# Value projections that leave the multiplier token by token, and latents that leave it unscaled

## The chip, the cores and the metric

The kernel runs on one core of one Trainium2 chip. A core has a matrix engine (TensorE, PE in the profile; its weight loads are shown apart as PEld), a vector engine (DVE), an activation engine (ACT), a general engine (POOL), and a queue engine (SP) that issues nearly all transfers. Each engine takes its instructions in a fixed order and stops at one that has to wait. Matrix products land in PSUM, eight banks of 128 x 512 float32; everything else is kept in SBUF or in device memory. The metric is the device time of one execution in microseconds (us); before the change the median of three runs is 2705.36 us (2704.07 to 2706.91).

## The reference

A two-layer encoder on 1024 tokens of width 1024. Each layer normalises x, projects it once, and cuts the columns of the projection among four attention groups; their outputs are concatenated, projected back and added; a squared-ReLU MLP follows. The parts that the change touches:

```
h = rms_norm(x, norm1_g[l]);  proj = h @ w_in[l]       # columns cut into groups A, B, C, D
A: cq (192), ckv (128), kr (32)                        # latents
   q = rms_norm(cq) @ w_uq;  c = rms_norm(ckv);  k_nope = c @ w_uk;  v = c @ w_uv
   softmax(q k) v, 4 heads of 64 + 32 rotary; values of 64
B: q, k (256 each, rotary), v (256 = 4 heads x 64)
   w = softmax(q1 k1) - lam * softmax(q2 k2);  w @ v
C: windowed attention, 4 query heads    D: neighbourhood attention on a 64-wide grid
```

Since `rms_norm` divides every token by its own root mean square (rms), the division may be done after a projection, and for `rms_norm(cq)` it drops out but for the small constant under the root.

## The kernel before

**Layout.** Activations are kept feature-major: a tile has 128 features on the partitions and 1024 tokens along the row. Every float32 operand is split into two parts, high and low (`split`: ACT writes the high part, DVE or POOL subtracts), and a product takes three matmuls: high x high, low x high, high x low (`passes`). In a projection the weights stand still in the array and 512 tokens move (`several`, `product`), so a tile of 128 output features takes 8 x 2 x 3 = 48 matmuls: eight pieces of the contraction, two halves of the tokens, three passes. The input of the projections is x times the gain, without 1/rms; that factor, spread over a tile `rb` along the tokens, is multiplied in when a result leaves PSUM (`ev_plain`), or is part of the rotary tables (`ev_rope`).

**Group B's start.** Two waves of three tiles each (`WAVES`) are projected into six PSUM banks: Q, K and V of heads 0 and 1, then of heads 2 and 3. ACT copies each half to SBUF (L453), which frees the bank. Q and K take a rotary step of three DVE products and a sum, a split into two `both` buffers' worth of parts (a pool of two), and a store to device memory. Attention needs values token-major, so `to_values` turns V: DVE multiplies by `rb`, PE transposes four pieces of 128 tokens into a bank (L642), ACT and DVE split the result, SP stores it. `attn_b` then loads Q, K and V per head (`stack`, `vtile`) and runs the softmax: scores into the `sb` banks (L810), scaling and row minimum on DVE (L812), the exponential on ACT (L815), transposes (L846) and products with V (L834, L835: the value tile stands still, 256 probabilities move).

**Latents.** While group B's attention runs, other work is put between its steps (`weave`, `fill`): `proj_latent` projects the three tiles of group A's latents, multiplies by `rb`, squares for the second norm (ACT, then matmuls against a column of ones, L659) and splits them; then `proj_d` projects group D. Group B's attention, latents and group D's projections all use a pool of two banks `mm`, two `tr`, three `sb` and one `pv`.

**Group A's values.** During group D's attention, `latent_up` projects the latents up; for the values it takes two tiles, each in two halves of 512 tokens (3 matmuls each), multiplies by a spread row `rkv` and turns the result with `to_values`.

**Order.** In the attention part a scheduler orders the instructions of each engine from their dependences and a model of their durations, with `high_priority` for steps of the attention; in the MLP the order of PE is that of the code.

## Time and profile before

| what | value |
|---|---|
| median of three runs | 2705.36 us |
| the profiled execution's own time | 2709.95 us |
| its span, first to last instruction | 2707.9 us |
| mean granted TensorE clock | 0.969 |
| PE, DVE, ACT, POOL busy | 94%, 72%, 53%, 42% of the span |
| layer 0: group B's projections and attention | about 30 to 350 us |
| layer 0: groups D, C and A's way up | about 350 to 480 us |
| layer 0: groups C and A, output projection | about 480 to 690 us |
| layer 0: MLP | about 690 to 1350 us |
| layer 1 | the same again from about 1350 us |

The busy time of PE adds matmuls that overlap, and a matmul's duration is longer than the time until the next one starts; so for what a matmul costs in a stream, the distance of two starts is read. A line such as `L190` is that of a helper (`tt`) and covers many uses; tiles tell them apart. The granted clock is the share of full speed at which the array ran in a stretch.

### The profile page before, as it was taken

The numbers are of one execution on the slowest core, as the hardware profiler recorded it, in microseconds if no ns is written. First come the engines' busy times: TensorE is split into PE (matmuls) and PEld (weight loads), VectorE is DVE, ScalarE is ACT, GpSimd is POOL, SyncE is SP. The second block draws the span as 40 slices with busy tenths as digits, with TensorE's granted clock in tenths as the row PEclk, the third lists the DMA queues.
The fourth block names the chain that finished last, engine by engine and source line by source line (L and its number), as shares of the span: only waits on it lengthen the run. The fifth ranks groups of instructions, "written<-read, shape, count | busy, mean of one in ns | idle before, by whom it ended". The sixth has DMA issues, their size and how long they took to land.

```text
span 2707.9 us, 37502 instructions
## 1 busy us (share of the span) xinstructions
PE 2549.6 (94%) x12296; PEld 2112.5 (78%) x12296; DVE 1943.0 (72%) x3379; ACT 1439.8 (53%) x2601; POOL 1130.9 (42%) x754
## 2 busy tenths in 40 slices
PE   8989988999899998999999999889998999999997
PEld 6778876787778887888877788668876788878886
DVE  6777866774966668887567777677749666688775
ACT  4667756664534444444436776566635344444444
POOL 2555642201345554545434656321013455544442
PEclk9989988999999999999998899899999999999998
DMA  5534597222144457444244446962221444664431
GB/s 175 169 107 129 158 287 239 82 89 63 46 144 148 153 170 267 143 142 141 95 139 134 121 113 183 295 202 69 71 71 52 154 153 152 221 221 146 136 105 63
DMA packets 186931, 389.19 MB, mean 144 GB/s; under 512 B 23712, under 2 KB 26736, under 8 KB 186736
## 3 DMA queue, kind: packets, MB, share of 16 engines
q1 hardware_dynamic: 172912, 361.62, 43.2%
q10 hardware_dynamic: 13824, 25.17, 2.7%
q8 instruction: 97, 1.59, 0.2%
q14 instruction: 98, 0.80, 0.1%
HBM read 263.29 MB, written 123.41 MB: 143 GB/s over the span
## 4 chain that ended last, share of the span: by engine, by line
PE 73%; DVE 12%; DMA 6%; ACT 4%; issue 3%; POOL 1%; SPq 0%; DVEq 0%; ACTq 0%; POOLq 0%
PE u L222 8%; PE u L224 8%; PE u L223 8%; PE mm L222 5%; PE mm L223 5%; PE mm L224 5%; PE p L222 5%; PE p L223 5%; PE p L224 5%; PE sb L810 3%; PE tr L846 3%; DVE p L812 2%; DVE part L190 2%; PE pv L835 2%; PE pv L834 2%
## 5 line engine op out<-in xcount | busy, mean ns | idle before, releaser
L190 POOL TENSOR_TENSOR wl<-raw,wh 128x512 fp32r<-128x512 f32 x448 | 632.8, 1413 | 704.8 <-ACT wh L196 691.0
L196 ACT ACTIVATE wh<-raw 128x512 fp32r<-128x512 f32 x448 | 281.5, 629 | 576.2 <-PE u L223 310.9
L190 POOL TENSOR_TENSOR wl<-ws,wh 128x512 fp32r<-128x512 f32 (+1 forms) x112 | 147.3, 1316 | 461.0 <-ACT wh L196 436.1
L222 PE MATMUL u<-far,wh 128*128 128x512 f32 x768 | 301.8, 393 | 11.4 <-ACT ev L1242 8.3
L224 PE MATMUL u<-far,wl 128*128 128x512 f32 x768 | 300.6, 391 | 2.2 <-POOL wl L190 2.2
L190 DVE TENSOR_TENSOR raw<-raw 128x512 f32<-128x512 f32 x256 | 223.1, 877 | 109.1 <-POOL wl L190 55.6
L223 PE MATMUL u<-far,wh 128*128 128x512 f32 x768 | 300.6, 391 | 0.0
L190 DVE TENSOR_TENSOR ptl<-tr,pth 128x512 fp32r<-128x512 f32 (+2 forms) x384 | 238.3, 629 | 68.5 <-ACT pth L196 66.8
L815 ACT ACTIVATE p<-p,nm 128x1024 f32<-128x1024 f32 x192 | 220.2, 1147 | 92.3 <-DVE nm L812 91.6
L196 ACT ACTIVATE pth<-tr 128x512 fp32r<-128x512 f32 (+2 forms) x384 | 205.2, 546 | 108.5 <-PE tr L846 64.9
L222 PE MATMUL p<-far,wh 128*128 128x512 f32 x640 | 252.9, 395 | 7.5 <-DVE ev L190 7.5
L224 PE MATMUL p<-far,wl 128*128 128x512 f32 x640 | 251.5, 393 | 1.5 <-POOL wl L190 1.5
L223 PE MATMUL p<-far,wh 128*128 128x512 f32 x640 | 252.2, 394 | 0.0
L810 PE MATMUL sb<-stack 96*128 96x512 f32 x640 | 217.5, 422 | 22.1 <-DVE nm L812 21.4
L190 DVE TENSOR_TENSOR far<-act,far 128x512 fp32r<-128x512 f32 x224 | 207.3, 955 | 14.7 <-ACT far L196 14.7
L190 POOL TENSOR_TENSOR p<-p 128x1024 f32<-128x1024 f32 x64 | 154.0, 2411 | 129.6 <-ACT p L898 121.3
L222 PEld LDWEIGHTS u<-far,wh 128*128 128x128 f32 x768 | 145.3, 189 | 43.5 <-ACT ev L1242 9.1
L222 PE MATMUL mm<-xh,wh 128*128 128x512 f32 x416 | 170.9, 411 | 0.8 <-DVE part L190 0.3
L224 PEld LDWEIGHTS u<-far,wl 128*128 128x128 f32 x768 | 145.2, 189 | 33.5 <-POOL wl L190 3.0
L812 DVE CUSTOM_DVE_ANT_0 p<-sb,zero,nm 128x512 f32<-128x512 f32 x192 | 142.4, 743 | 37.7 <-PE sb L810 34.6
L223 PEld LDWEIGHTS u<-far,wh 128*128 128x128 f32 x768 | 145.4, 189 | 30.0
L223 PE MATMUL mm<-xl,wh 128*128 128x512 f32 x416 | 167.7, 403 | 0.0
(245 smaller groups left out, 6110.1 us busy)
## 6 DMA issues: line engine op xcount, KB each, us to landing
act<-acts SPq DMA_DIRECT2D x224, 256.0 KB
raw<-in_w_up SPq DMA_DIRECT2D x128, 256.0 KB
acts<-ev SPq DMA_DIRECT2D x128, 256.0 KB
raw<-in_w_down SPq DMA_DIRECT2D x128, 256.0 KB
acts<-ev ACTq DMA_DIRECT2D x96, 256.0 KB
ws<-in_w_in SPq DMA_DIRECT2D x76, 256.0 KB
rz<-drows SPq DMA_DIRECT2D x40, 256.0 KB
stack<-kd SPq DMA_DIRECT2D x32, 256.0 KB
```

The lines of the kernel that those rows point to most:

```text
L190: (eng or self.nc.vector).tensor_tensor(out=out, in0=a, in1=b, op=op)
L196: nc.scalar.activation(hi, src, AF.Copy)
L222: mm(ps, w[0], x[0][:, sl], start=start, stop=False)
L223: mm(ps, w[0], x[1][:, sl], start=False, stop=False)
L224: mm(ps, w[1], x[0][:, sl], start=False, stop=stop)
L810: self.nc.tensor.matmul(ps, q[:, qt * P:(qt + 1) * P], k[:, sl], start=i == 0, stop=i == len(passes) - 1)
L812: self.nc.vector.tensor_tensor_reduce(out=p[:, sl], in0=ps, in1=self.zero[:, 0:1].bitcast(F).broadcast_to([P, 512]), scale=-scale, scalar= ...
L815: self.nc.scalar.activation(p, p, AF.Exp, bias=nm[:, 1:2], scale=-1.0, accum_out=z)
L834: nc.tensor.matmul(out, v[:, kt], h[:, sl], start=kt == 0, stop=False)
L835: nc.tensor.matmul(out, v[:, kt], lo[:, sl], start=False, stop=kt == 7)
L846: nc.tensor.transpose(t[:, k * 256 + i * P:k * 256 + (i + 1) * P], p[:, (j * 2 + k) * P:(j * 2 + k + 1) * P], self.ident)
```

## The change

**Group B's values.** The tiles for V are gone from the input tiles, and their 256 columns are given as an array of their own, `w_val`. The first wave is Q and K of heads 0 and 1 and Q of heads 2 and 3 (`FIRST`); the second is K of heads 2 and 3, as before, and V of all four heads. V is computed token-major: 128 tokens of x stand still, 256 weight columns move (`token_major`), eight token tiles, two to a bank, four banks. `keep_values` splits a bank in two steps of 256 columns, with the factor 1/rms of the token as a scale per partition (`rtok`), and stores it in one transfer. No transposes, no copy to SBUF and no product with `rb` are left for these values.

**Group A's values.** The same way: eight token tiles, two to a bank, each three matmuls with 256 moving columns, and `keep_values` with the scale from `rows[1]`.

**Latents.** They leave PSUM without `rb`: ACT squares the bank and writes the high part, DVE the low part, straight from PSUM. The 1/rms of x comes back by three small products on 128 x 16 columns: twice on the sums of squares, once on the result. The rotary key keeps its tables.

On PE, layer 0, the second wave. Before, V's transposes of the first wave (`tr<-ident,part`) stand among the matmuls of 512 columns (`sb`, `tr`, `pv` are banks, `xh` and `xl` the parts of x, `wh` and `wl` those of the weights):

```order
L222 MATMUL sb<-xh_180,wh 128x512
L223 MATMUL sb<-xl_181,wh 128x512
L222 MATMUL sb<-xh_180,wh 128x512
L223 MATMUL sb<-xl_181,wh 128x512
L642 MATMUL tr<-ident,part 128x128 x8
L224 MATMUL sb<-xh_180,wl 128x512 x2
L222 MATMUL sb<-xh_184,wh 128x512
```

Now (L254 is the matmul of `token_major`; its first name is what moves, its second what stands still):

```order
L228 MATMUL sb<-xh_172,wh 128x512
L254 MATMUL sb<-wh,xh_164 128x256
L254 MATMUL sb<-wh,xl_165 128x256
L229 MATMUL sb<-xl_173,wh 128x512
L254 MATMUL tr<-wh,xh_164 128x256
L254 MATMUL tr<-wh,xl_165 128x256
```

The transposes are gone; matmuls of half the width, with parts of x standing still, have taken the place of those for Q and V.

On ACT, at the end of the second wave, before (L453 copies out of PSUM, L815 exponential, L646 the high part of V, L656 the square of a latent):

```order
L453 ACTIVATE p<-tr 128x512 x2
L196 ACTIVATE wh<-ws 128x512
L453 ACTIVATE p<-pv 128x512
L196 ACTIVATE both<-part 128x512
L815 ACTIVATE p,z_779<-p,nm 128x1024
L196 ACTIVATE both<-part 128x512
L815 ACTIVATE p,z_780<-p,nm 128x1024
L646 ACTIVATE both<-tr 128x8x64
L656 ACTIVATE part<-part 128x512
```

and now (L201 the high part of V, L866 exponential, L698 square):

```order
L201 ACTIVATE both<-sb,rtok 128x4x64
L201 ACTIVATE both<-tr,rtok 128x4x64
L198 ACTIVATE wh<-ws 128x512
L201 ACTIVATE both<-sb,rtok 128x4x64
L201 ACTIVATE both<-tr,rtok 128x4x64
L866 ACTIVATE p,z_851<-p,nm 128x1024
L201 ACTIVATE both<-tr,rtok 128x4x64
L698 ACTIVATE part<-mm 128x512
L201 ACTIVATE both<-pv,rtok 128x4x64
L201 ACTIVATE both<-tr,rtok 128x4x64
L866 ACTIVATE p,z_852<-p,nm 128x1024
L201 ACTIVATE both<-pv,rtok 128x4x64
```

All of V is now split after the second wave, in two pairs of `both` buffers, with the first exponentials between them.

On SP, the stores and the first load of group B's values, before:

```order
L169 DMA vb<-both 128x2x512
L162 DMA stack<-kb 32x1024 x3
L169 DMA vb<-both 128x2x512
L162 DMA stack<-qb 32x1024
L162 DMA stack<-kb 32x1024
L162 DMA stack<-qb 32x1024
L162 DMA stack<-kb 32x1024
L162 DMA stack<-qb 32x1024
L162 DMA stack<-kb 32x1024
L162 DMA v<-vb 128x1024
L162 DMA ws<-in_w_in 128x512
```

and now:

```order
L164 DMA ws<-in_w_in 128x512 x2
L171 DMA vb<-both 128x4x256 x4
L164 DMA ws<-in_w_in 128x512
L164 DMA v<-vb 128x1024 x2
L171 DMA kb<-both 64x2x512 x4
L164 DMA ws<-in_w_in 128x512
```

Two stores of V with other loads between them and the first load of V have become four stores in a row, behind the loads of Q and K, with both loads of V one row behind them.

The diff, cut to its core (left out: the list of column tiles, signatures, and names that only follow):

```diff
@@ -29,9 +29,9 @@
 
 
 T_CQ, T_CQR, T_CKV = 0, 1, 2
-T_BQ, T_BK, T_BV = (3, 6), (4, 7), (5, 8)
-T_DQ, T_DK, T_DV = (9, 12), (10, 13), (11, 14)
-T_CQ2, T_CK, T_CV = (15, 16), 17, 18
+T_BQ, T_BK = (3, 5), (4, 6)
+T_DQ, T_DK, T_DV = (7, 10), (8, 11), (9, 12)
+T_CQ2, T_CK, T_CV = (13, 14), 15, 16
 
 
 def input_tiles():
...
@@ -109,6 +109,8 @@
     out = host_constants()
     out["x"] = i["x"][0].T.reshape(8, P, S)
     out["w_in"] = tiles_of(padded(i["w_in"], 2)[:, :, np.concatenate(input_tiles())], 4)
+
+    out["w_val"] = i["w_in"][:, :, 864:1120].reshape(n, 4, 2, P, 256).transpose(0, 1, 3, 2, 4)
 
     wo = i["w_out"].reshape(n, 8, P, DM)[:, [2, 3, 6, 7, 4, 5, 0, 1]].reshape(n, DM, DM)
     out["w_out"] = tiles_of(wo, 4)
...
@@ -210,6 +213,9 @@
         wh, wl = keep if keep is not None else (
             pool.tile([P, wide, P], R, tag=tag + p, bufs=bufs, name=tag + p)[:, :n] for p in "hl")
         self.split(wh, wl, st, eng=self.nc.gpsimd)
+        if wide_rows:
+            flat = [v.rearrange("p k c -> p (k c)") for v in (wh, wl)]
+            return [tuple(v[:, k * 256:k * 256 + 256] for v in flat) for k in range(n // 2)]
         return [(wh[:, k], wl[:, k]) for k in range(n)]
 
     def wtile(self, src):
...
@@ -238,6 +244,15 @@
                     for n in range(2):
                         self.passes(b[n], w[k], xs[4 * c + k], slice(n * 512, n * 512 + 512),
                                     c == 0 and k == 0, c == 1 and k == 3)
+
+    def token_major(self, ps, at, x, w, tile, start=True, stop=True):
+
+
+        cols = slice(tile * P, tile * P + P)
+        o = ps[:, at:at + 256]
+        for i, (a, b) in enumerate(((0, 0), (1, 0), (0, 1))):
+            self.nc.tensor.matmul(o, x[a][:, cols], w[b], start=start and i == 0, stop=stop and i == 2,
+                                  skip_group_check=True)
 
 
     def rsqrt_cols(self, ss, count):
...
@@ -438,26 +449,47 @@
                     def wave():
                         return [(self.bank(a), self.bank(b)) for a, b in (("sb", "sb"), ("sb", "tr"), ("tr", "pv"))]
 
+                    def evict(ev, banks):
+                        raw = self.ptile()
+                        for n in range(2):
+                            sl = slice(n * 512, n * 512 + 512)
+                            nc.scalar.activation(raw[:, sl], banks[n], AF.Copy)
+                            ev(n, raw[:, sl])
+
                     banks = wave()
                     self.several(first, xs, banks, ahead)
                     acc = self.squares(self.x, self.ap, "p", self.NP)
+                    rtok = self.col("rtok", 8)
                     with tc.high_priority(offset=200):
-                        self.spread_here(rb, self.rstd_cols(acc, DM, self.ones[:, 0:1]))
+                        r = self.rstd_cols(acc, DM, self.ones[:, 0:1])
+                        nc.vector.tensor_copy(rtok, r)
+                        self.spread_here(rb, r)
                     tabs = self.table("32", rb, nc.vector)
                     self.eng = nc.vector
-                    for t in range(2):
-                        for ev, b in zip(evacs_b(t), banks):
-                            raw = self.ptile()
+                    rope = lambda dst: self.ev_rope(tabs, dst)
+                    for dst, b in zip((qb[:, 0], kb[:, 0], qb[:, 1]), banks):
+                        evict(rope(dst), b)
+
+                    banks = wave()
+                    vbanks = banks[1] + banks[2]
+                    for c in range(2):
+                        wk = self.weights(w_in(T_BK[1])[c])
+                        wv = [w for i in range(2) for w in self.weights(
+                            d["w_val"][l, 2 * c + i].rearrange("p k (a c) -> p (k a) c", c=P), wide_rows=True)]
+                        for k in range(4):
+                            begin, end = c == 0 and k == 0, c == 1 and k == 3
                             for n in range(2):
-                                sl = slice(n * 512, n * 512 + 512)
-                                nc.scalar.activation(raw[:, sl], b[n], AF.Copy)
-                                ev(n, raw[:, sl])
-                        if t == 0:
-                            banks = wave()
-                            self.several([w_in(t) for t in self.WAVES[1]], xs, banks)
-                        self.eng = nc.gpsimd
-
-                    fill = chain(self.proj_latent(l, one, xs, rb, tabs, lat, krd, rows), proj_d())
+                                self.passes(banks[0][n], wk[k], xs[4 * c + k], slice(n * 512, n * 512 + 512),
+                                            begin, end)
+                            for t in range(8):
+                                self.token_major(vbanks[t // 2], t % 2 * 256, xs[4 * c + k], wv[k], t,
+                                                 begin and t % 2 == 0, end)
+                    for i, b in enumerate(vbanks):
+                        self.keep_values(b, vb, 2 * i, rtok)
+                    self.eng = nc.gpsimd
+                    evict(rope(kb[:, 1]), banks[0])
+
+                    fill = chain(self.proj_latent(l, one, xs, rtok, tabs, lat, krd, rows), proj_d())
                     self.weave(chain.from_iterable(self.attn_b(l, t, qb, kb, vb, y["b"]) for t in range(2)),
                                fill, self.RB, self.LB, every=self.EV[0])
                     self.tails.append(self.mix_b(mix, y["b"], self.gsub[:, l:l + 1]))
...
@@ -539,7 +571,7 @@
 
     EV = (.5, .5, .7, 1)
     EARLY, RC, RA, LA = 4, (8, 1), (3, 1), 0
-    WAVES = [(T_BQ[t], T_BK[t], T_BV[t]) for t in range(2)]
+    FIRST = T_BQ[0], T_BK[0], T_BQ[1]
     NP, RB, RD, LB, LD = 6, (7, 8), (3, 2), 40, 50
 
     def weave(self, main, fill=iter(()), ratio=(1, 0), lead=0, end=True, every=1):
...
@@ -632,12 +664,22 @@
             self.emit_parts(y, [(dst[:, :, sl].rearrange("a p s -> p a s"), slice(0, P))], scale=scale)
         return then
 
-    def to_values(self, dst, tag="mm"):
+    def keep_values(self, ps, dst, k0, r):
+
+
+        b = self.both()
+        v = b.rearrange("p a b -> p (a b)").rearrange("p (h k e) -> p h k e", h=4, k=2)
+        for k in range(2):
+            src = ps[:, k * 256:k * 256 + 256].rearrange("p (h d) -> p h d", h=4)
+            self.split(v[:, :, k, 0:64], v[:, :, k, 64:128], src, r[:, k0 + k:k0 + k + 1])
+        self.keep(dst[:, :, k0:k0 + 2].rearrange("h p k e -> p h k e"), v.bitcast(F))
+
+    def to_values(self, dst):
 
         nc = self.nc
 
         def then(n, y):
-            ps = self.bank(tag)
+            ps = self.mm_ps()
             for k in range(4):
                 nc.tensor.transpose(ps[:, k * P:(k + 1) * P], y[:, k * P:(k + 1) * P], self.ident)
             src = ps.rearrange("p (k h d) -> p h k d", k=4, h=2)
...
@@ -670,13 +712,13 @@
         both = cols[:, 0:16]
         squares = [cols[:, i * 8:i * 8 + 8] for i in (0, 2, 1)]
         for i, t, g in ((0, T_CQ, self.gq[:, l, 0:1]), (2, T_CKV, self.gkv[:, l:l + 1])):
-            yield from one(t, xs, self.ev_plain(rb, lambda n, y: self.latent_parts(y, g, P, n, lat[:, i], squares[i])))
+            yield from one(t, xs, lambda n, y: self.latent_parts(y, g, P, n, lat[:, i], squares[i]))
         c, s = tabs
 
         def ev(n, ps):
             sl = slice(n * 512, n * 512 + 512)
             y, t2 = self.part(), self.part()
-            self.tt(y[0:64], ps[0:64], rb[0:64, sl])
+            self.latent_parts(ps, self.gq[:, l, 1:2], 64, n, lat[:, 1], squares[1])
             self.tt(y[64:112], ps[64:112], c[64:112, sl])
             self.tt(t2[64:80], ps[96:112], s[96:112, sl])
             self.tt(t2[96:112], ps[64:80], s[64:80, sl])
...
@@ -685,14 +727,19 @@
             self.emit_parts(y[64:112], [
                 (krd[:, :, h, sl].rearrange("a p s -> p a s"), slice(64 + 32 * h, 80 + 32 * h))
                 for h in range(2)], slice(64, 112))
-            self.latent_parts(y, self.gq[:, l, 1:2], 64, n, lat[:, 1], squares[1])
 
         yield from one(T_CQR, xs, ev)
         q, k = squares[0], squares[2]
         self.tt(q, q, squares[1], ALU.add)
 
         nc.vector.tensor_scalar(k, k, 192 / 128, None, ALU.mult)
-        rows_out.append(self.rows_of(self.rsqrt_cols(both, 192)))
+        twice = lambda v: v.rearrange("p (g t) -> p g t", g=2)
+        rx = rtok.rearrange("p (o t) -> p o t", o=1).broadcast_to([P, 2, 8])
+        for _ in range(2):
+            self.tt(twice(both), twice(both), rx)
+        r = self.col("rlat", 16)
+        self.tt(twice(r), twice(self.rsqrt_cols(both, 192)), rx)
+        out += [self.rows_of(r), r[:, 8:16]]
         yield True
 
     def latent_up(self, l, lat, rows, qa, ka, va):
...
@@ -733,9 +780,13 @@
         yield from two([w0[2], both(w0[3])], parts[0:2], plain(rq, qn[:, 0]))
         w1 = self.weights(d["w_lat"][l, 1])
         yield from two(w1[2:3], parts[2:3], plain(rkv, kn[:, 0]))
-        w2 = self.weights(d["w_lat"][l, 2])
-        for t in range(2):
-            yield from two(w2[t:t + 1], parts[2:3], self.ev_plain(rkv, self.to_values(va[2 * t:2 * t + 2])))
+        w2 = self.weights(d["w_lat"][l, 2], wide_rows=True)
+        for i in range(4):
+            ps = self.mm_ps()
+            for k in range(2):
+                self.token_major(ps, k * 256, parts[2], w2[0], 2 * i + k)
+            self.keep_values(ps, va, 2 * i, rows[1])
+            yield True
         yield from two([w1[0], both(w1[1])], parts[0:2], plain(rq, qn[:, 1]))
         yield from two(w1[3:4], parts[2:3], plain(rkv, kn[:, 1]))
 
```

13 lines of the change are left out of this document (5 added, 8 removed).

## The prediction

> **What bounds the kernel now.** First the page's busy times and the chain's shares by engine, then the windows around group B's attention (layer 0: 84 to 350 us, layer 1: 1430 to 1700 us) and group D's stage, whose columns are length, busy time of PE, PEld, DVE, ACT and POOL, the granted clock, DMA share and GB/s:
>
> ```profile
> PE 2549.6 (94%) x12296; PEld 2112.5 (78%) x12296; DVE 1943.0 (72%) x3379; ACT 1439.8 (53%) x2601; POOL 1130.9 (42%) x754
> PE 73%; DVE 12%; DMA 6%; ACT 4%; issue 3%; POOL 1%; SPq 0%; DVEq 0%; ACTq 0%; POOLq 0%
> ...
> 84.00:186.00 102.00, 90.06 (x436) 73.32 (x435) 80.81 (x190) 70.10 (x115) 59.83 (x34) 0.88 0.42 124
> 186.00:350.00 164.00, 163.03 (x915) 140.09 (x914) 123.26 (x320) 120.61 (x206) 94.42 (x55) 1.00 0.51 146
> 350.00:480.00 130.00, 107.76 (x549) 88.38 (x547) 85.68 (x228) 81.51 (x212) 40.47 (x25) 0.88 0.84 255
> 1430.00:1530.00 100.00, 93.05 (x452) 76.64 (x453) 76.13 (x194) 72.03 (x117) 56.29 (x30) 0.86 0.39 114
> 1530.00:1700.00 170.00, 168.23 (x925) 143.06 (x924) 120.39 (x319) 122.06 (x211) 92.67 (x54) 0.99 0.53 153
> ```
>
> Group B's attention has two parts. In the later one PE is busy 163.0 of 164 us and 168.2 of 170: the fill work (latents, group D) keeps it full, so PE work that goes away shortens the span. At the head PE idles 11.9 and 7.0 us and its clock falls to 0.88 and 0.86. There it waits for DVE (waits of PE, us in total, times, longest; 84 to 200 us, then 1350 to 1600):
>
> ```profile
> PE sb L810 <- DVE nm L812: 8.2, 5, 4.6
> ...
> PE sb L810 <- DVE nm L812: 8.3, 8, 3.9
> ```
>
> Group D's stage, into which group A's values fall, is held otherwise: PE 83% busy, DMA 84%, and its piece of the chain is made of transfers:
>
> ```profile
> 352.60 9.21 DMA rq<-drows
> 361.82 10.88 DMA latp<-lat
> ...
> 412.38 8.37 DMA va<-both
> ```
>
> **The change part by part: the matmuls.** What a matmul costs in a stream is read from starts: PE's timeline, the first and last of 15 matmuls of 512 columns, and one run of eight of 256 columns (products with V, each with its own weight load) behind eight transposes and a score matmul:
>
> ```profile
> 79.70 0.39 PE L222 MATMUL pv<-xh,wh 128*128 128x512 f32 x1
> ...
> 82.87 0.39 PE L224 MATMUL pv<-xh,wl 128*128 128x512 f32 x1
> ...
> 186.25 1.04 PE L846 MATMUL tr<-ident,p 128*128 128x128 f32 x8
> 187.04 0.47 PE L810 MATMUL sb<-stack 96*128 96x512 f32 x1
> 187.35 0.28 PE L834 MATMUL pv<-pth,v 128*128 128x256 f32 x1
> ...
> 188.19 0.28 PE L835 MATMUL pv<-ptl,v 128*128 128x256 f32 x1
> ```
>
> 512 columns: 3.17 / 14 = 0.226 us. 256 columns: 0.84 / 7 = 0.120. A transpose: 0.79 / 8 = 0.099. Per layer, group B's values go from 2 tiles x 48 = 96 matmuls (21.74 us) and 16 transposes (1.58) to 8 x 8 x 3 = 192 (23.04): -0.28 us, all in stages where PE is full or runs without a gap. Group A's go from 12 matmuls (2.72) and 16 transposes (1.58) to 24 (2.88): -1.42 us, in group D's stage; since PE waits for other things a sixth of that stage and transfers lead the chain, I take half, -0.71, between nothing and the whole. Both layers: -0.56 and -1.42.
>
> The price of 0.120 is the row that the sum hangs on. The new matmuls are alike in shape (128 stationary columns, 256 moving, a weight load each) but always change what stands still; in the run above the value tile changes with every second one and the starts show no difference. Its weight loads last
>
> ```profile
> L834 PEld LDWEIGHTS pv<-pth,v x40: 186/189/337, 109.6 to 194.9; 128*128 128x128 f32 x40
> ```
>
> 0.189 us each, longer than the 0.120 between starts, so they overlap. If nothing overlapped, the pitch would be 0.189: 432 matmuls x 0.069 = +29.8 us in both layers; that is the far bound. The Trainium skill speaks against the change here: "TensorE: Matmul & The Clock Gate", section Back-to-back issue gap, puts a stream of load and matmul pairs at about 81 ns for 128 columns and 131 ns for 512, so half the width would cost much more than half. Interpolated, an estimate of 98 ns for 256, group B's values would take 192 x 0.098 = 18.8 against 96 x 0.131 = 12.6 us. The trace doesn't agree: 0.226 for 512, and 0.120, about half, for 256.
>
> **Stalls before the transposes.** PE stopped in front of V's transposes within a wave, once in each layer:
>
> ```profile
> 60.52 1.26 PE L642 MATMUL tr<-ident,part 128*128 128x128 f32 x8 [1.58 <-DVE part L190]
> 1396.85 1.97 PE L642 MATMUL tr<-ident,part 128*128 128x128 f32 x8 [2.17 <-DVE part L190]
> ```
>
> Both go: 3.75 us. What is late next are the scores, which wait for DVE's rotary steps of K, and those don't come earlier unless K's copies do. I take half, -1.9.
>
> **DVE.** Groups of instructions with what one costs (mean ns before the bar's end; `part<-p,rb` scales V, `both<-tr` splits it; the 256-column row is the nearest to the new split steps; ACT's row is the copy for V's high part, and the same at 256):
>
> ```profile
> L190 DVE TENSOR_TENSOR part<-mm,rb 128x512 f32<-128x512 f32 x12 | 8.2, 684 | 0.2 <-PE mm L224 0.2
> L190 DVE TENSOR_TENSOR part<-p,rb 128x512 f32<-128x512 f32 x8 | 6.2, 819 | 0.0
> L190 DVE TENSOR_TENSOR both<-tr,both 128x512 fp32r<-128x512 f32 x8 | 5.5, 686 | 13.4 <-ACT both L646 13.4
> L190 DVE TENSOR_TENSOR ptl<-tr,pth 128x256 fp32r<-128x256 f32 x32 | 13.4, 417 | 5.7 <-ACT pth L196 5.7
> ...
> L646 ACT ACTIVATE both<-tr 128x512 fp32r<-128x512 f32 x8 | 4.8, 594 | 14.9 <-DMA kb<-both 14.8
> L196 ACT ACTIVATE pth<-tr 128x256 fp32r<-128x256 f32 x32 | 11.8, 376 | 10.6 <-PE tr L991 10.6
> ```
>
> Per layer the latents lose six products with `rb` (four full halves, two of 64 rows, at 0.684): 4.1 us at the head. Group B's values lose 4 x 0.819 + 4 x 0.686 = 6.0 and get 8 x 0.417 = 3.3; but half of the old steps (3.0) stood under the second wave and all the new ones stand at the head, +0.3 there. The head is relieved of 3.8 us a layer. At least nothing of it becomes time, at most all (PE idles more than that); V's steps now stand in front of the second score step, the lost products lay further back. I take half, -3.8 in both layers. Q of heads 2 and 3 is turned a wave earlier, with sums and splits on DVE instead of POOL, 4 x 0.686 = 2.7 us more, beside the second wave's matmuls:
>
> ```profile
> 30.00:84.00 54.00, 50.94 (x233) 41.46 (x233) 34.15 (x43) 15.24 (x31) 17.29 (x12) 1.00 0.59 163
> ```
>
> PE is busy there, DVE 63%: 0, and 5.4 in both layers if K's steps were pushed back by it. ACT loses four copies out of PSUM and four of the 0.594, and gets 8 x 0.376; nothing waits for it first: 0. Group A's values trade four products and four splits at about 0.68 for 8 x 0.417 on a DVE that is 66% busy in group D's stage: 0.
>
> **What it adds.** Four tiny steps a layer (a copy of 8 columns, three products of 16); of their kind:
>
> ```profile
> L190 DVE TENSOR_TENSOR rs_t<-rs_t,ms 128x16 f32<-128x16 f32 x6 | 4.4, 736 | 0.4 <-ACT rs_t L253 0.3
> ```
>
> 8 x 0.736 = 5.9 us if each stood on the path; mostly they stand between score steps. I take +1.0.
>
> A latent's bank in `mm` is now held for a square, a scaled copy and a subtraction instead of one product, and an exponential may stand between:
>
> ```profile
> L656 ACT ACTIVATE part<-part 128x512 f32<-128x512 f32 x8 | 5.0, 622 | 1.9 <-DVE part L190 1.9
> L199 ACT ACTIVATE both<-part,par 128x512 fp32r<-128x512 f32 x8 | 5.7, 709 | 0.0
> L200 DVE SCALAR_TENSOR_TENSOR both<-part,par,both 128x512 fp32r<-128x512 f32 x8 | 8.6, 1076 | 1.8 <-ACT both L199 1.8
> L815 ACT ACTIVATE p<-p,nm 128x1024 f32<-128x1024 f32 x192 | 220.2, 1147 | 92.3 <-DVE nm L812 91.6
> ```
>
> 2.4 us, with the exponential 3.6, against 0.68. Behind a late bank wait the next half's matmuls, and behind these in PE's order the next scores. What covers it is the other half in the second bank, 24 x 0.226 = 5.4 us: 0 while that holds, 12 halves x 2.9 = +34 us if never.
>
> Stores of V have runs of half the length, 1 KB. A packet's time went with its bytes so far (queue 1 over the span, then from 340 to 480 us; packets, MB, share of 16 engines):
>
> ```profile
> q1 hardware_dynamic: 172912, 361.62, 43.2%
> ...
> q1 hardware_dynamic: 13828, 35.64, 83.5%
> ```
>
> 0.108 us for 2.09 KB and 0.135 for 2.58 KB, 52 ns per KB both: 0. If each of the 1024 further packets of group A in a layer cost half of 0.135, it would be 4.3 us of all 16 engines in a stage that transfers lead.
>
> **The sum:** -0.56 - 1.42 - 1.9 - 3.8 + 1.0 = -6.7 us. The profiled execution took 2709.95 us (span 2707.9), so 2703.3 for such a one, and 2705.36 - 6.7 = 2698.7, **2699**, for the median, which lay 4.6 below it. A change within 0.2%, 5.4 us, can hardly be told from none: the forecast lies just beyond.
>
> **The rivals.**
>
> *The head closes up.* DVE's 7.6 us count whole, with the stalls (3.75) and PE's 3.4, less 1.0, 13.8 us; and the clock, 1.00 where PE has no gaps and 0.88 and 0.86 at the heads, rises by a third of the way: 183 us of PE's busy time there x 0.04 = 7.3. -21, **2684**. For it: the waits for L812 above. Against it: the rest of the waits is the scores' own.
>
> *The gaps close up again.* Group A's part lies under transfers, the scores wait for K as before, and only group B's 0.56 and a little of DVE's relief is left: **2704**. For it: the chain rows of 352 to 420 us; what is saved at the head meets the same rotary steps.
>
> *Values come late.* Slower. All of V is split after the second wave, stored, and loaded just before its first use, which PE reached at
>
> ```profile
> 82.11 0.81 DVE L190 TENSOR_TENSOR part<-p,tabc 128x512 f32<-128x512 f32 x1 [4.46 <-ACT p L453]
> ...
> 88.60 3.25 DVE L190 TENSOR_TENSOR part<-p,tabs 64x512 f32<-64x512 f32 x2
> ...
> 109.64 0.38 PE L834 MATMUL pv<-pth,v 128*128 128x256 f32 x1
> ...
> 63.36 4.20 DMA kb<-both
> ```
>
> The rotary steps of K, 82.1 to 91.9, stand in front of the second splits. First pair ready at 91.9, stored by 96.1 (4.20 as for `kb`), second pair 2 us later, stored by 102.3, loaded by 106.5: 3.1 us before 109.64. With 8.37 us a transfer, as for `va` above, it is 91.9 + 8.4 + 2 + 8.4 + 8.4 = 119.1, 9.5 us late, and everything behind the first product with V on PE waits: 2 x 9.5 - 6.7 = +12.3, **2718**. It decides once the three transfers take more than 5.2 us each. Behind the loads in SP's queue stand K's stores and weights of the next latent, so those would be late too. Against it: DMA is 42% busy at the head.
>
> *Pairs have a fixed part.* A line through 0.099 (128 columns) and 0.226 (512) gives 0.141 for 256: 432 x 0.021 = +9.1, with the rest +2.4, so **2708**. Against it stands the measured 0.120. The Trainium skill's "TensorE: Matmul & The Clock Gate", Back-to-back issue gap, has such a fixed part.
>
> **How the numbers follow.** Forecast 0.46, its own range 2692 to 2706; head closed up 0.17; gaps close 0.17; values late 0.15; fixed part 0.05. Of the forecast's 0.46, 0.28 lie below 2700, 0.16 within 0.2%, 0.02 above; the first rival is all faster; the second 0.03, 0.13 and 0.01; late values 0.01 within and 0.14 slower; the fixed part 0.01 and 0.04. Faster 0.48, same 0.31, slower 0.21. The range 2683 to 2716 takes in the first rival's time and the late values up to 8.5 us a layer, and leaves out about half of each, under 0.2 in all; it does not reach the bounds of +34 and +29.8, which rows speak against.
>
> **What would show it.** The new matmuls (`sb`, `tr`, `pv` from weights and `xh`) starting 0.120 us apart; no stall within the second wave; a shorter head with fewer PE waits for L812 and a later part still full; V loaded before PE reaches its first product. A wait of PE for `v`, or for `mm` banks held by latents, or starts above 0.13 apart, would make it wrong, and so would a stage that the change doesn't touch coming out longer.

## The result and the profile after

The changed kernel takes 2738.19 us (median of four runs, 2736.34 to 2743.98) against 2706.14 for the kernel before in the same comparison: 1.0119 times as long, 95% interval 1.0097 to 1.0141. It is slower by 32 us, where 2699 was forecast, and lies outside the range. The profiled execution has a span of 2734.9 us, 27.0 more than before. Run times are medians of executions at the usual granted clock; one of f_vfirst below, 4144 us at 0.554, is left out.

First the page's busy times, then the windows that were shown of before, with the same columns:

```profile
PE 2558.2 (94%) x12448; PEld 2118.3 (77%) x12448; DVE 1927.1 (70%) x3383; ACT 1438.8 (53%) x2609; POOL 1113.8 (41%) x746
...
84.00:186.00 102.00, 85.67 (x410) 69.08 (x410) 75.11 (x200) 72.25 (x121) 55.73 (x32) 0.87 0.46 134
186.00:350.00 164.00, 163.15 (x892) 138.53 (x890) 115.59 (x306) 115.88 (x196) 92.69 (x54) 1.00 0.47 136
350.00:480.00 130.00, 106.00 (x558) 88.98 (x557) 86.43 (x229) 83.39 (x219) 40.36 (x26) 0.87 0.86 260
1430.00:1530.00 100.00, 85.30 (x416) 69.04 (x414) 70.44 (x176) 68.29 (x114) 53.10 (x31) 0.88 0.52 150
1530.00:1700.00 170.00, 166.06 (x885) 139.10 (x886) 124.07 (x329) 121.17 (x203) 94.77 (x55) 0.98 0.43 125
```

DVE, ACT and POOL have less to do than before, as meant. PE, which also has less, is busy 8.6 us longer. At group B's head it is busy 85.7 of 102 us, where it was 90.1.

Fixed windows mix stages that have moved. So the span is cut by PE's own steps: group B from its first score to group D's first, groups D and C from there to the last score of C, group A from there to its last score. Before, layer 0 and then layer 1:

```profile
83.10:330.00 246.90, 234.00 (x1233) 196.13 (x1232) 191.39 (x474) 177.11 (x288) 142.81 (x82) 0.95 0.44 129
330.00:480.00 150.00, 127.76 (x669) 106.42 (x667) 99.25 (x264) 96.01 (x245) 52.80 (x33) 0.90 0.85 255
480.00:614.50 134.50, 128.64 (x786) 109.85 (x785) 102.59 (x236) 88.30 (x161) 15.95 (x10) 1.00 0.28 82
1420.10:1669.10 249.00, 237.93 (x1231) 198.28 (x1230) 187.84 (x476) 178.38 (x289) 144.16 (x81) 0.94 0.44 126
1669.10:1820.00 150.90, 126.21 (x677) 105.41 (x675) 100.53 (x265) 96.33 (x243) 52.79 (x35) 0.92 0.87 256
1820.00:1953.00 133.00, 127.11 (x780) 109.06 (x779) 100.22 (x232) 87.81 (x160) 13.83 (x9) 1.00 0.29 82
```

And the changed kernel:

```profile
81.70:330.10 248.40, 231.61 (x1197) 192.36 (x1198) 179.16 (x472) 176.39 (x290) 138.10 (x78) 0.95 0.43 127
330.10:478.90 148.80, 124.42 (x664) 104.99 (x663) 99.76 (x260) 96.45 (x248) 52.97 (x34) 0.89 0.88 260
478.90:627.20 148.30, 138.11 (x812) 117.18 (x811) 108.09 (x241) 90.92 (x164) 21.09 (x12) 0.96 0.29 82
1433.50:1683.10 249.60, 232.96 (x1191) 192.12 (x1191) 182.07 (x472) 177.25 (x290) 137.33 (x78) 0.94 0.44 129
1683.10:1837.70 154.60, 125.38 (x685) 104.11 (x684) 98.70 (x263) 96.38 (x249) 51.74 (x35) 0.91 0.85 247
1837.70:1979.00 141.30, 133.96 (x800) 114.53 (x798) 107.07 (x238) 90.89 (x163) 21.15 (x12) 0.98 0.31 86
```

The account of the 27.0 us: the waves end 1.4 sooner; the three stages together are 14.1 longer in layer 0 (531.4 to 545.5) and 12.6 in layer 1; what follows them takes 0.7 and 1.0 more. By kind, over the six stages: PE idles 104.6 us where it idled 82.7 (length less busy), +21.9, and is busy 986.4 where it was 981.7, +4.8, at a lower granted clock in group A. Group B is hardly longer (+1.5 and +0.6), but PE has less to do in it; groups D, C and A together are 12.6 and 12.0 longer. Group A's attention has not one changed operation, and it is 13.8 and 8.3 longer. Other work fills PE there, the early half of the output projection, whose input is the tile `mixh`. The first of the three kinds of matmul on `mixh`, with number, shortest, median and longest time, and first and last start, before (layers 0 and 1) and in the changed kernel; the early half comes first:

```profile
L222 PE MATMUL mm<-mixh,wh x104: 387/390/628, 465.2 to 695.7; 128*128 128x512 f32 x104
L222 PE MATMUL mm<-mixh,wh x104: 388/390/499, 1800.9 to 2035.4; 128*128 128x512 f32 x104
...
L228 PE MATMUL mm<-mixh,wh x104: 389/389/628, 485.7 to 708.4; 128*128 128x512 f32 x104
L228 PE MATMUL mm<-mixh,wh x104: 389/389/628, 1835.4 to 2060.8; 128*128 128x512 f32 x104
```

Before, it began 14.8 and 19.1 us ahead of group C's last score (480.0 and 1820.0), where PE has gaps. Now it begins 6.8 us behind it and 2.3 ahead (478.9 and 1837.7), and of group A's further 13.8 and 8.3 us PE is busy for 9.5 and 6.9.

### The profile page after: what moved, and what is told of

The parts are those of the page before. It is cut to its first block, busy times and chain, and to the rows that moved or that the text cites. A ratio compares the mean times of both kernels' runs of the same rounds, so it can differ in the third digit from the quotient of the medians.

```text
span 2734.9 us, 37799 instructions
## 1 busy us (share of the span) xinstructions
PE 2558.2 (94%) x12448; PEld 2118.3 (77%) x12448; DVE 1927.1 (70%) x3383; ACT 1438.8 (53%) x2609; POOL 1113.8 (41%) x746
## 3 DMA queue, kind: packets, MB, share of 16 engines
q1 hardware_dynamic: 177008, 361.62, 43.1%
## 4 chain that ended last, share of the span: by engine, by line
PE 71%; DVE 13%; DMA 7%; ACT 4%; issue 3%; POOL 1%; SPq 1%; DVEq 0%; ACTq 0%; POOLq 0%
PE u L228 8%; PE u L230 8%; PE u L229 8%; PE mm L228 5%; PE mm L229 5%; PE mm L230 5%; PE p L228 5%; PE p L229 5%; PE p L230 5%; PE sb L861 3%; PE tr L897 2%; DVE p L863 2%; DVE part L192 2%; PE pv L886 2%; PE pv L885 1%
## 5 line engine op out<-in xcount | busy, mean ns | idle before, releaser
L866 ACT ACTIVATE p<-p,nm 128x1024 f32<-128x1024 f32 x192 | 220.3, 1148 | 104.5 <-DVE nm L863 92.1
L192 POOL TENSOR_TENSOR p<-p 128x1024 f32<-128x1024 f32 x64 | 152.9, 2393 | 120.5 <-ACT p L949 104.6
L897 PE MATMUL tr<-ident,p 128*128 128x128 f32 x1024 | 164.8, 279 | 7.2 <-DVE ptl L192 3.7
```

Of the source, the lines that this page charges most:

```text
L192: (eng or self.nc.vector).tensor_tensor(out=out, in0=a, in1=b, op=op)
L866: self.nc.scalar.activation(p, p, AF.Exp, bias=nm[:, 1:2], scale=-1.0, accum_out=z)
L897: nc.tensor.transpose(t[:, k * 256 + i * P:k * 256 + (i + 1) * P], p[:, (j * 2 + k) * P:(j * 2 + k + 1) * P], self.ident)
```

## The experiments

Two things were to be told apart: a cost that the change's own operations have, and the price of a new order. A scheduler deals the instructions of the attention anew for every edit: of TensorE's 12088 matmuls and transposes in the program before, 280 are gone, and about four fifths of the others are left in the same sequence.

### The change in parts

Each kernel is the one before with one part of the change:

```
b_only:     group B's values token-major; latents and group A's values as before
lat_only:   latents unscaled, three small products; both value projections as before
aval_only:  group A's values token-major; latents scaled by rb
a_only:     lat_only + aval_only
```

> Only group B's values are projected token-major (second wave, its evictions and stores); latents and group A's values are as before. Theory 'stores' (group A's value stores in 1 KB runs delay the loads of groups D and C, where transfers already lead): this part has no such store in that stage, so the forecast's own terms hold, 2706 - 2 to 2706 - 4, about 2703. Theory 'latents' (the unscaled latents and their three multiplications delay what hangs on them): the same 2703, since latents are untouched. Theory 'order' (any edit makes the scheduler deal the instructions of the later groups anew, and the new deal is worse): anything from 2695 to 2730, with a changed time in the stages of groups D, C and A, in which this kernel has no changed operation.

> Only the latents leave PSUM unscaled, with the three small multiplications; both value projections are as before. Theory 'stores': 2705, within 3 of before. Theory 'latents': most of the 32 us, 2725 to 2740, lost between the last latent load and the last group A score. Theory 'order': anything from 2695 to 2730, not tied to the latents' own stage.

> Only group A's values are projected token-major, in four banks with stores of 1 KB runs; latents are scaled as before, group B as before. Theory 'stores': most of the 32 us, 2725 to 2740, with the DMA engines busy for longer in the stage of groups D and C. Theory 'latents': 2703 to 2706. Theory 'order': anything from 2695 to 2730.

> Both edits of group A (unscaled latents, token-major values), group B as before. Theories 'stores' and 'latents': the sum of the two single edits within 4 us, 2730 to 2741. Theory 'order': not the sum; it may miss it by 10 us or more either way.

Measured: 2726.44, 2732.76, 2716.80 and 2716.82 us against 2704.76, ratios 1.0078 [1.0052, 1.0104], 1.0100 [1.0079, 1.0122], 1.0040 [1.0027, 1.0054] and 1.0045 [1.0030, 1.0061]. Every part alone is slower, and they don't add up: latents +28 and values +12 make +12 together. "Stores" falls, since the latents' part has no changed store and loses most. "Latents" falls, since their loss is gone when group A's values are changed too. What stays is "order", or costs that cover each other; lat_only lies 3 us above the range that "order" was given.

One thing does follow a part. The 50 us from some 2 to 5 us ahead of group B's first score, layers 0 and 1, with the windows' columns; first the kernel before:

```profile
80.00:130.00 50.00, 46.31 (x219) 37.34 (x217) 38.71 (x85) 35.62 (x58) 27.17 (x16) 0.90 0.51 160
1417.00:1467.00 50.00, 45.79 (x193) 36.55 (x191) 35.76 (x80) 31.90 (x52) 25.88 (x16) 0.83 0.51 155
```

Then the latents' part alone:

```profile
80.00:130.00 50.00, 47.59 (x233) 39.09 (x232) 35.70 (x86) 36.17 (x60) 28.26 (x17) 0.93 0.52 165
1425.00:1475.00 50.00, 47.14 (x245) 38.55 (x244) 38.47 (x95) 38.19 (x63) 30.50 (x18) 0.97 0.52 159
```

Then group B's values alone:

```profile
80.00:130.00 50.00, 40.52 (x179) 29.91 (x178) 34.94 (x82) 31.37 (x54) 22.17 (x13) 0.83 0.57 167
1428.00:1478.00 50.00, 42.27 (x191) 32.17 (x190) 35.07 (x84) 32.53 (x55) 24.25 (x14) 0.83 0.53 159
```

And the whole change:

```profile
80.00:130.00 50.00, 41.09 (x177) 32.13 (x176) 32.96 (x82) 32.32 (x55) 23.51 (x14) 0.83 0.56 165
1431.00:1481.00 50.00, 40.78 (x171) 31.80 (x170) 32.53 (x80) 31.68 (x55) 21.41 (x13) 0.83 0.56 169
```

In these kernels PE is busy for 41 to 42 of 50 us with group B's values token-major, and for 45 to 48 without (aval_only 47.0 and 45.0, a_only 47.6 and 46.6). The whole change loses 5.2 and 5.0 us there, and DVE is less busy too. An order can undo the loss, though: with lead 44, below, the changed kernel has 41.5 and 45.9, and the kernel before 47.0 and 44.1.

### Another order of the same instructions

The first two are the kernel before, the others the changed one. No instruction is added or taken away, only the priority or the place of some steps is another, so that the scheduler deals another order (`LB` is the lead of group B's steps over the work put between them):

```
-    NP, RB, RD, LB, LD = 6, (7, 8), (3, 2), 40, 50
+    NP, RB, RD, LB, LD = 6, (7, 8), (3, 2), 36, 50      # n_lb36; 44 in n_lb44, a_lb44
-    EV = (.5, .5, .7, 1)
+    EV = (.5, 1, .7, 1)                                 # a_ev_d1
```

> The kernel before with one number changed, the lead of group B's steps over the fill in the scheduler's priorities, 40 to 36. Every engine has the same instructions as before (12088 rows of TensorE); 1392 of them, 599 of VectorE's and 83 of SyncE's transfers stand in another order, from group B's stage on. Theory 'order' (the 32 us are the price of a new order, whatever the edit): 2715 to 2735, in the range of the single edits, with 5 or more us of TensorE idle time per layer added. Theory 'work' (each edit has a cost of its own in the stages of groups D, C and A): 2701 to 2710, the same as before.

> The same with the lead at 44: again the same instructions, 1597 of TensorE's in another order. Theory 'order': 2715 to 2735. Theory 'work': 2701 to 2710.

> The changed kernel with the lead of group B's steps at 44 in place of 40: the changed kernel's instructions, 1899 rows of TensorE in another order. Theory 'order': its time moves by 10 us or more from 2738, more likely down (2705 to 2728), since 2738 is the worst of the five orders timed so far. Theory 'work': 2730 to 2745.

> The changed kernel with the tails (group B's and group D's normalisation and mixing steps) taken at every step of group D's stage instead of every second one: the same instructions, group B's second pair of outputs is stored sooner, which releases the tile that VectorE waited 6.4 us for. Theory 'late tail' (the late store of group B's outputs is what makes the stage of groups D and C and the start of group A long): 2710 to 2725, with the wait for that store gone and group D's matmuls of the output projection starting within 15 us of before's 465. Theory 'order': any time from 2705 to 2740, with or without that wait. Theory 'work': 2730 to 2745.

Measured: 2708.56, 2728.47, 2731.96 and 2749.25 us against 2707.46, ratios 1.0002 [0.9987, 1.0017], 1.0073 [1.0050, 1.0096], 1.0084 [1.0063, 1.0106] and 1.0150 [1.0127, 1.0173]. So an order alone can cost 21 us, and need not: lead 36 costs nothing. The range given for "order" held for n_lb44 alone: n_lb36 lies in that of "work", a_lb44 moved by 6 us and not by 10 or more, and a_ev_d1 is above all ranges. "Late tail" falls: the second store of group B's outputs is issued at 386.0 us in place of 411.5, and VectorE's wait for it is no longer among those of 3 us or more, but the output projection starts at 490.7, not sooner, and the kernel is 11 us slower than the changed one. Where the kernel before loses its 21 us at lead 44 (16.3 in the profiled execution), cut as above:

```profile
83.50:332.20 248.70, 235.43 (x1231) 194.78 (x1230) 189.35 (x476) 178.22 (x288) 141.61 (x81) 0.95 0.43 128
332.20:486.70 154.50, 128.55 (x664) 107.74 (x663) 98.14 (x260) 93.93 (x240) 48.10 (x31) 0.87 0.84 241
486.70:623.60 136.90, 130.56 (x794) 111.30 (x792) 107.34 (x236) 90.87 (x163) 20.76 (x12) 1.00 0.31 87
1428.10:1674.40 246.30, 235.10 (x1231) 196.82 (x1230) 189.80 (x476) 180.49 (x290) 143.66 (x82) 0.95 0.44 130
1674.40:1826.20 151.80, 127.97 (x664) 105.86 (x663) 96.71 (x260) 93.60 (x240) 48.18 (x31) 0.88 0.86 244
1826.20:1967.70 141.50, 132.93 (x793) 112.32 (x792) 107.35 (x236) 90.57 (x165) 20.74 (x12) 0.99 0.31 86
```

In the same places as the change does: groups D, C and A are 6.9 and 9.4 us longer than before (291.4 and 293.3 against 284.5 and 283.9), and the output projection starts late too, at 483.2 and 1822.7, 3.5 us ahead of group C's last score in both layers.

### Banks held at the split

In the chain of waits of the changed kernel at the head (start, us, what), a store of values must land before ScalarE goes on, and a store of K before another latent half leaves its bank:

```profile
90.47 3.37 DMA vb<-both
...
94.30 0.60 ACT part L698
94.94 1.86 PE mm L701 x8
...
106.27 6.09 DMA kb<-both
...
112.44 0.70 ACT both L201
113.16 0.76 DVE both L202
113.97 1.87 PE mm L701 x8
```

Every split that leaves for device memory goes into one of two `both` buffers, and a buffer is free when its store has landed. Before, a copy or a product freed the bank first. That was tried in four kernels: group B's banks copied to SBUF by ScalarE ahead of the split (a_raw), a third buffer, for which one of the three `part` buffers gave the room (a_both3), the latents copied by VectorE (lat_copy, on lat_only), and both copies (a_lcopy_raw). The lines are shortened:

```
+    nc.scalar.activation(raw[:, half], vbanks[2 * i + n], AF.Copy)      # a_raw: keep_values reads raw
-    tag="both", bufs=2      tag="part", bufs=3                          # a_both3
+    tag="both", bufs=3      tag="part", bufs=2
+    y = self.part(); nc.vector.tensor_copy(y, ps)                       # lat_copy: latent_parts reads y
```

> The changed kernel, in which ScalarE first copies the four banks of group B's values to SBUF as they are (as the banks beside them), and the split with the scale reads that copy. Theory 'hold' (the split needs one of two buffers that come free only when a store has landed, and until then it holds the bank, its engine and so the scores behind it): TensorE's busy time from 80 to 130 us returns from 41.1 to 46 or more of 50 (46.3 before), the same in layer 1, and the whole takes 8 to 12 us less than 2738, 2726 to 2730. Theory 'order' (which instruction stands where, whatever holds it): the head of group B stays at 40 to 43 of 50, or the total moves by some other amount, 2710 to 2750.

> The changed kernel with three of the buffers through which every split leaves, in place of two (and two in place of three of the buffers for parts, to make room). Theory 'hold': the head of group B comes back by half or more (44 to 47 of 50 between 80 and 130 us) and the total falls to 2715 to 2730. Theory 'order': head and total are not tied; 2710 to 2750.

> Only the latents are left without the multiplier, as in the single edit that took 2733, but VectorE first copies each bank to SBUF, where before it multiplied, and the split reads that copy. Theory 'hold': the bank is released as soon as before, so the 28 us of that edit go: 2703 to 2712. Theory 'order': the copy takes as long as the product and frees the bank as early, but 1892 of TensorE's rows stand elsewhere than before: 2705 to 2735, the middle likelier than the lower end.

> The changed kernel with both copies: group B's values and the latents leave PSUM by a copy, and are split from SBUF; group A's values are split from PSUM, as their transposes were before. Theory 'hold': the terms of the forecast hold again, 2700 to 2712. Theory 'order': 2710 to 2745, with no more than group B's head back.

Measured: 2742.77, 2710.90, 2740.94 and 2730.20 us against 2706.97, ratios 1.0133 [1.0114, 1.0152], 1.0017 [1.0006, 1.0028], 1.0117 [1.0100, 1.0134] and 1.0082 [1.0066, 1.0099]. The copies free the banks and bring nothing: PE's busy time at the head stays at 41.9 and 42.2 of 50 in a_raw, and the latents are no faster with their copy than without. "Hold", as it was put, falls; lat_copy is 6 us above what either theory allowed. The third buffer takes 27 us off, 4 more than "hold" had said, but gives the head back only 1.2 and 2.5 us. What it does bring back is group A's stage, 131.8 and 132.0 us: the output projection starts 23.3 and 22.0 us ahead of group C's last score.

### Late values, and a control for the third buffer

Before, the load of head 0's values was issued at 73.15 us and the first product with them stood at 109.64 (timeline of SP's queue):

```profile
73.15 0.38 SPq L162 DMA_DIRECT2D v<-vb  x1
```

In the changed kernel (timeline, SP's queue and PE):

```profile
104.49 0.81 SPq L164 DMA_DIRECT2D v<-vb  x2
...
116.27 0.41 PE L885 MATMUL pv<-pth,v 128*128 128x256 f32 x1
```

f_vfirst computes all values of group B at the start of the second wave and K of heads 2 and 3 behind them (shortened):

```
-    vbanks = banks[1] + banks[2]          # K on banks[0], its matmuls between those of the values
+    vbanks = banks[0] + banks[1]          # K on banks[2], all its matmuls behind keep_values
```

> The changed kernel with the second wave in another order: all of group B's values first, on the banks that held Q and K of heads 0 and 1, then K of heads 2 and 3 on the other two, so that the values leave while 48 matmuls of K (some 11 us) still run. Theory 'late values': head 0's values are loaded by 95 us in place of 104.5, the first product with them starts at 105 to 111 us in place of 116.3, TensorE is busy for 44 to 47 of the 50 us from 80 on, and the total falls by 8 to 12, to 2726 to 2730, if the later stages stay. Rival 'order': the head comes back or not, and the later stages move by as much again, 2705 to 2750.

> The same with three buffers for splits and two for parts. If late values and buffers are two causes of the change's loss, 2698 to 2704, below before. Rival 'order': no sum of the two gains, 2700 to 2735.

> The kernel before with three buffers for splits and two for parts. Theory 'buffers' (the change needs the splits' buffers more than the kernel before does, so a third one gives back the change's loss): 2700 to 2708, the same as before within 3 us or so. Rival 'buffers help both': 2680 to 2690, 20 or more below, and the change's own loss stays as large. Rival 'order': up to 2735, since this too deals the instructions anew.

> The changed kernel with three buffers for splits and two for parts, and the lead of group B's steps at 44 in place of 40: another order of the same instructions. Theory 'buffers': 2705 to 2717, near 2711 whatever the order. Rival 'order': 2711 was one lucky order, and this one is at 2718 to 2740.

Measured: 2732.83, 2710.16, 2729.48 and 2720.12 us against 2705.98, ratios 1.0103 [1.0084, 1.0123], 1.0022 [1.0012, 1.0032], 1.0084 [1.0062, 1.0106] and 1.0050 [1.0033, 1.0066]. The timeline of f_vfirst, and its heads:

```profile
94.29 0.82 SPq L164 DMA_DIRECT2D v<-vb  x2
...
110.85 0.28 PE L882 MATMUL pv<-pth,v 128*128 128x256 f32 x1
```

```profile
80.00:130.00 50.00, 43.82 (x209) 35.69 (x209) 31.25 (x83) 34.49 (x56) 23.78 (x15) 0.90 0.58 183
1426.00:1476.00 50.00, 42.69 (x191) 33.57 (x191) 31.44 (x81) 31.82 (x54) 21.48 (x13) 0.90 0.65 197
```

The values come 10 us sooner, the first product 5.4 us sooner (2.5 of them because the first score stands at 79.2 in place of 81.7), and PE gets 2.7 and 1.9 us back of the 5.2 and 5.0 lost; with the third buffer as well 3.3 and 3.9 (44.38 and 44.68 of 50). Counted from 3 us ahead of its own first score, layer 0 of f_vfirst has 42.5 of 50, which is 1.4 back. The edit also brings a wait of its own: between 80 and 120 us PE stands 3.9 us for a load of K, which the changed kernel does not. So late values are a likely cause of the head's loss, for a quarter to a half of it; this edit does not set them apart from everything else that it moves. The total gains 5 us, not 8 to 12: groups D, C and A moved again, and so did the rest of group B. Against "buffers" and "buffers help both" alike, the kernel before gets 24 us slower with the third buffer.

### Pairs

Two last runs completed pairs with the same setting on both sides:

> The changed kernel with the lead of group B's steps at 36: the same instructions, 1760 of TensorE's rows in another order; the kernel before at this lead takes 2709. Theory 'order' (each setting deals the later groups anew, and the change's own cost is small beside that): 2710 to 2745 with no tie to the 32 us of lead 40. Theory 'work' (the change costs some 30 us whatever the order): 2735 to 2742. In both, group B's head stays at 40 to 44 of 50 us, because the values of head 0 are still the last to leave.

> The kernel before with three buffers for splits, two for parts, and the lead at 44; the changed kernel takes 2720 there. Theory 'order': 2705 to 2740, on either side of 2720. Theory 'work' (the change costs some 30 us): 2685 to 2695. Theory 'buffers' (with a third buffer the change is the faster kernel): 2725 to 2735.

Measured: 2749.16 and 2710.22 us against 2705.87, ratios 1.0150 [1.0128, 1.0171] and 1.0013 [0.9996, 1.0029]. The first is above the ranges of both theories, the second within that of "order". All pairs, medians in us (the differences are taken before rounding):

| setting | kernel before | changed kernel | difference |
|---|---|---|---|
| lead 40, as given | 2706 | 2738 | +32 |
| lead 36 | 2709 | 2749 | +41 |
| lead 44 | 2728 | 2732 | +3 |
| third split buffer, lead 40 | 2729 | 2711 | -19 |
| third split buffer, lead 44 | 2710 | 2720 | +10 |

"Work", 30 us whatever the order, falls with the last three rows, "buffers" with the last one. The mean of the five is +13 us and their spread (standard deviation) 24, so an interval of 95% around the mean is about 29 either way: what the change costs on the mean over orders can't be told from nothing by these pairs. With two split buffers all three are on the slower side. No version tried beats the kernel before.

## Why the prediction was wrong

**The sum.** This is the step that failed: it adds the terms to the profiled time as if all other instructions kept their places. The scheduler orders by dependences and modelled durations, so they didn't, and the same instructions in other orders take 2706 to 2728 us before the change and 2732 to 2749 after it. A sum of -6.7 is small beside that. The last paragraph of the prediction named the sign, a stage that the change doesn't touch coming out longer; it should have been a rival with a price. What makes one order of groups D, C and A slower than another is settled only in part. One regularity runs through all 20 profiles, cut at the same steps: in the 26 stages where the output projection starts 12.9 us or more ahead of group C's last score, group A's stage takes 131.6 to 135.2 us; in the 14 where it starts 3.5 us ahead or later, 136.9 to 155.0. In the changed kernel this is 22.1 of the 27.0 us. No run moved that start by itself, so it is not shown as a cause, and what sets the start is open: transfers take a share of 0.84 to 0.88 of groups D and C in all three kernels shown, and one suspected wait, the late store of group B's outputs, was taken away without gain. Nor is it all that an order can do: the kernel before with a third buffer starts the projection 22 us ahead in both layers and loses more than its 24 us in groups D and C, which take 168 us in each layer in place of 150 and 151.

**DVE, -3.8.** Not seen in the whole change. DVE was relieved: it is busy 33.0 and 32.5 of the head's 50 us, before 38.7 and 35.8. PE waits for it less too (waits of PE, us in total, times, longest, from 84 to 200 us):

```profile
PE sb L861 <- DVE nm L863: 3.8, 10, 0.9
PE mm L701 <- ACT part L698: 2.9, 1, 2.9
PE sb L861 <- DVE both L202: 2.3, 1, 2.3
```

But PE's busy time at the head fell by 5.2 and 5.0 us. The waits that had seemed to hold the head were not all that its length hung on, and new ones stand beside them. The sign of the term by itself is not settled: in lat_only, which loses the products with `rb` and keeps the early values, PE is 1.3 and 1.4 us busier at the head, but lead 44 alone moves the kernel before there by +0.7 and -1.7.

**Values come late**, 0.15 and 2718, was half right. The first product stands 6.6 us later than before, between the rival's 3.1 early and 9.5 late, and f_vfirst speaks for a share of it in the head's loss. But PE doesn't wait for `v` in the profile: the scheduler puts scores and other work ahead of the product, so the sign that was named, V loaded before PE reaches its first product, could not have shown it.

**Matmuls.** Right. Six of the new matmuls in a row, first and last start:

```profile
68.03 0.28 PE L254 MATMUL pv<-wh,xh 128*128 128x256 f32 x1
...
68.63 0.28 PE L254 MATMUL pv<-wl,xh 128*128 128x256 f32 x1
```

0.60 / 5 = 0.120 us, as taken. The rival of a fixed part per pair falls. The rule that the prediction weighed there (the Trainium skill's "TensorE: Matmul & The Clock Gate", Back-to-back issue gap) doesn't fit this trace either.

**Stalls before the transposes**, half of 3.75. Right in size: the first score comes 1.4 us sooner in layer 0, where this half and group B's matmuls made 1.2 a layer. Both stalls are gone; in their wave PE now waits 1.3 and 1.2 us for weights to be split, where it waited 1.2 and 0.5. In layer 1 nothing of the gain shows: from the MLP's first product to the first score it is 721.6 us, before 721.0.

**Q of heads 2 and 3 on DVE, 0.** Right: DVE stands idle for 12.3 us ahead of K's steps at 81.64.

**ACT, and the latents' banks, 0 and 0 with a bound of +34.** Too low: at the head PE waits 2.9 us for ACT's square of a latent (L698), which ACT takes up only after a split that waited for its buffer; in layer 1 it waits 2.8. That is some 6 us, where the kernel before waited 1.7 and 0.6 for the same step, so 3.4 more. But removing the hold by copies brought no time. (The bound, 12 x 2.9, is 35.)

**Group A's matmuls, -1.42, and the tiny steps, +1.0** can't be seen beside changes of 10 us in their stage.

**Stores of 1 KB, 0.** About right: queue 1 has 4096 packets more and took 43.1% of 2734.9 us where it took 43.2% of 2707.9, 1179 against 1170 us of 16 engines, within some 3 us of rounding. The latents' edit, without such stores, loses more than the stores' edit.

## What to carry to other kernels

Where a scheduler orders the instructions, an edit is also a new deal, and its price is measured by dealing the same work again with another priority: here up to 21 us in a kernel of 2700, several times the 6.7 that the edit was expected to bring. A setting that suits one kernel need not suit the next (the third split buffer took 27 us off the changed kernel and cost the kernel before 24), so before and after are to be compared over several settings each, and an edit worth a few us can't be judged by one build. Work that fills another stage's gaps is worth following by its start: where it came late here, the next stage was longer by as much as 20 us. When results are produced in one piece instead of two, ask what their first reader now waits for: here the first head's values left a wave later, and a lighter VectorE did not make up for what the head lost.

## What was not expected of the hardware

That a gap of PE is paid twice was known from the clocks at the heads, but not how sharply. Windows of 5 us of the changed kernel (PE's busy time second, granted clock third from the end):

```profile
85.00:90.00 5.00, 3.29 (x15) 2.39 (x13) 4.89 (x9) 1.36 (x3) 3.47 (x2) 1.00 0.87 190
90.00:95.00 5.00, 1.03 (x3) 0.43 (x3) 2.68 (x8) 2.20 (x4) 1.27 (x1) 0.85 0.78 262
95.00:100.00 5.00, 5.00 (x16) 4.32 (x17) 4.67 (x16) 3.67 (x7) 0.00 (x0) 0.50 0.32 102
100.00:105.00 5.00, 5.00 (x23) 4.06 (x22) 0.74 (x4) 3.11 (x5) 1.99 (x2) 0.96 0.37 113
```

After 5.7 us without work out of 10, the longest stop among them 2.9 us, PE runs the next 5 us without a gap at 0.50, and then at 0.96. The Trainium skill's "TensorE: Matmul & The Clock Gate", Part 1: The HAM clock gate, has the like: half the clock after an idle stretch of about 3.4 us, and the whole again after as much steady work. Here the idle stretch had a few short matmuls in it, and the steady work took some 5 us. Over the six stages the changed kernel's PE is busy 4.8 us longer with nearly 3 us less work (group A's matmuls, 2 x 1.42), so by this estimate close to 8 of its 27 us are matmuls at a lower clock; most of the rest is idle time.
